# A hybrid decoder layer on one core: TensorE keeps the source's order in the stage of the state-space groups, and the weave of that stage is rewritten

## The chip, the cores and the metric

The kernel runs on 1 core of one Trainium2 chip. The time is device time in microseconds from one launch. The kernel before was timed in three runs, 1043.99, 1045.71 and 1045.89 us, with a median of 1045.71 us. One more execution was taken with the hardware profiler; it took 1044.05 us, of which 1042.2 us lie between its first and its last instruction (the span).

## The reference

One decoder layer on 512 tokens of width 1024, with 16 learned meta tokens ahead of them. All data are fp32.

```python
u = rmsnorm(h, mix_norm_w)
proj = u @ w_in                       # pool | z | xbc | dt | gates
y_pool = pool_mixer(u_pool) @ w_pool_up
y_ssd = mamba2_branch(z, xbc, dt) @ w_ssd_out
h = h + (gate_pool * y_pool + gate_ssd * y_ssd) @ w_o
v = rmsnorm(h, mlp_norm_w)
h = h + (relu(v @ w_ff1) ** 2) @ w_ff2
out = rmsnorm(h, final_norm_w)[16:]
...
# mamba2_branch
xbc = silu(causal_depthwise_conv(xbc))        # x (2048) | B (8x128) | C (8x128)
y = ssd_chunked(x, dt, a, B, C) + x * d_skip  # 4 chunks of 128 tokens, 8 groups
y = y * silu(z)
y = y * rsqrt(mean(y * y over the group's 256 channels) + eps) * norm_w
```

In `ssd_chunked`, for each group of four heads and each chunk, C and B give a masked 128x128 matrix that is weighted by exponentials of summed dt and applied to x (the part inside the chunk), and a running state, built from B and x chunk by chunk, is applied by C (the part from earlier chunks).

## The kernel before

Channels lie on the 128 partitions, tokens along the free dimension. Each fp32 product is made from three products of rounded halves: a weight block of 128x1024 is loaded (`raw`, on SyncE's queue, three buffers), ScalarE copies its rounded upper half (`whi`, L75) and VectorE subtracts to get the lower half (`wlo`, L76), each of the two with four buffers; `proj` (L147 to L153) then issues per 128 rows of the contraction the products whi by upper half (L150), whi by lower half (L151) and wlo by upper half (L153). A projection of 528 tokens takes 48 matmuls into one accumulator of two banks (`px`, L150 to L153), one of 512 tokens 24.

The stage that the change touches is a loop over eight groups g (L577). For each g, `ssd(g)` (L390) is a generator of seven steps, and its steps alternate with those of the projections for the next group, `group_proj(g + 1)` (L359): B (`bt`), C (`ct`) and the two halves of x (`xc`), each a block of 48 matmuls with a convolution of four taps behind it (L340 on ScalarE, L343 three times on VectorE, L345 the Silu on ScalarE), then in some groups a pooling gate (`pgp`, 24 matmuls), then z (`pz`, two blocks, 48 matmuls in all, Silu on ScalarE at L385). In group 4 the first half of the output projection (`pso`, 192 matmuls in eight steps) comes first; in group 7 there is no next group, and the step's partner is the second part of the output projection (`psp`, eight steps of 18 matmuls).

The seven steps of `ssd(g)` are these.

1. TensorE transposes B into `ptb`, the meta tokens of x into `ptm` and x into `ptx` (L407 to L428). ScalarE copies `btok` and the rounded meta tokens `bm` (L409 to L413), VectorE finishes `bm` (L414), and makes `xm`, `xdt` and `xdd` (L418 to L433). The decay factors `eb` and `abc` are exponentials on ScalarE (L439 to L450) with subtractions on both engines.
2. TensorE makes `pcb` from B and C (L455) and the state increments `pst` (L462 for the meta tokens, L464). VectorE masks `pcb` into `cbm` (L457), multiplies it into `abc` (L470, 128x2048) and runs the states: `st` of chunk 1, 2 and 3, each a product (L468) and an addition (L469) on the state before; chunk 0 is a copy on ScalarE (L466).
3. TensorE makes `po`, two halves of four chunks each, from the states (L478), and `py` from `abc` and `xdt` (L484). VectorE combines them into `yt` for the first half (L488 to L492).
4. The same four operations on VectorE for the second half.
5. ScalarE squares `yt` (L496); the square is split into `qh` and `ql`.
6. TensorE sums the squares over the group's channels (`png`, L501 and L502), ScalarE takes the root (L504), VectorE four reciprocals (L506).
7. VectorE scales `yt` (L510), and the result is split into `yh` (L513, ScalarE) and `yl` (L514, VectorE), which the output projections read.

What each engine issues first is not set by this text alone. The layer under the kernel records the operations with their dependencies and gives each engine one fixed sequence, by priorities in the order of the source and by its own estimate of when an operation can start; the tiles' buffers are handed out along with it. Each engine then works through its sequence in order and waits on semaphores. In the kernel before this holds for all engines: TensorE's sequence, too, is the scheduler's, which put matmuls of a following block between the products of `po`, or the whole of z ahead of transposes.

The accumulators of two banks (`psum2`) have two buffers, those of one bank (`psum1`) four.

Of the kernel before, what the change touches and what calls it, by code (L numbers as in the profile page):

```python
# [21 lines left out]
G = 8  # L22
# [19 lines left out]
GATE_AT = {1: 3, 2: 4, 3: 5, 5: 6}  # L42
# [9 lines left out]
def kernel(ctx: ExitStack, tc, xT, x, w, vec, fnw, out):  # L52
# [12 lines left out]
    def block_tiles():  # L65
        b = nblk[0]
        nblk[0] += 1
        return (b, wp.tile([P, 1024], F32, tag="raw", name=f"raw{b}", bufs=3),
                wp.tile([P, 1024], F32R, tag="whi", name=f"whi{b}"),
                wp.tile([P, 1024], F32R, tag="wlo", name=f"wlo{b}"))  # L70

    def block_part(t, c):
        b, raw, hi, lo = t
        nc.sync.dma_start(raw[:, c], w[b, :, c])
        act.copy(hi[:, c], raw[:, c])  # L75
        dve.tensor_tensor(lo[:, c], raw[:, c], hi[:, c].bitcast(F32), op=ALU.subtract)  # L76

    def block():
        t = block_tiles()
        block_part(t, slice(0, 1024))  # L80
        return t[2:]

    def units():

        while True:
            hi, lo = block()
            for j in range(NK):
                yield hi[:, j * P : (j + 1) * P], lo[:, j * P : (j + 1) * P]

    def mm3(ps, a, b, first, last):  # L90
        (ah, al), (bh, bl) = a, b
        pe.matmul(ps, ah, bh, start=first, stop=False)  # L92
        pe.matmul(ps, ah, bl, start=False, stop=False)  # L93
        pe.matmul(ps, al, bh, start=False, stop=last)  # L94
# [45 lines left out]
    def psum2(name):  # L140
        return psa.tile([P, 1024], F32, tag="mm", name=name)
# [4 lines left out]
    def proj_step(outs, k, wblk, rhs):  # L146

        wh, wl = (t[:, k * P : (k + 1) * P] for t in wblk)
        for o, c in outs:
            pe.matmul(o, wh, rhs[0][k][:, c], start=k == 0, stop=False)  # L150
            pe.matmul(o, wh, rhs[1][k][:, c], start=False, stop=False)  # L151
        for o, c in outs:
            pe.matmul(o, wl, rhs[0][k][:, c], start=False, stop=k == NK - 1)  # L153

    def proj(outs, wblk, rhs):
        for k in range(NK):
            proj_step(outs, k, wblk, rhs)

    def wide(ps, skip=0):

        h = (L - skip) // 2
        runs = [(ps[:, 512 - h : 512], slice(skip, skip + h)),
                (ps[:, 512 : 512 + h], slice(skip + h, L))]
        return runs, ps[:, 512 - h : 512 + h]

    def narrow(ps):
        return [(ps, slice(NM, L))]
# [20 lines left out]
    b, raw, hi, lo = wdt  # L188
# [89 lines left out]
    def dtile(name):  # L278
        return dp.tile([P, W], F32, name=name)

    v, e, s, s2, pl, dt, acs = (dtile(n) for n in ("dv", "de", "ds", "ds2", "dpl", "ddt", "dacs"))
# [22 lines left out]
    for c in (slice(0, P), slice(P, W)):  # L304
        n = c.stop - c.start
# [31 lines left out]
    def conv(dst, src, ct):  # L337
        n = dst.shape[-1]
        e = src.shape[-1] - n
        act.activation(dst, src[:, e:], AF.Identity, bias=col(V_CB, ct), scale=col(V_CW, ct * 4 + 3))  # L340
        for j in range(1, 4):
            o = max(0, j - e)
            dve.scalar_tensor_tensor(dst[:, o:], src[:, e + o - j : e + n - j],  # L343
                                     col(V_CW, ct * 4 + 3 - j), dst[:, o:], op0=ALU.mult, op1=ALU.add)
        act.activation(dst, dst, AF.Silu)  # L345

    def group_tiles(g):
        xc = gc.tile([P, 2, L], F32, tag="xc", name=f"xc{g}")
        bt = gc.tile([P, L], F32, tag="bt", name=f"bt{g}")
        ct = gc.tile([P, SEQ], F32, tag="ct", name=f"ct{g}")  # L350
        zt = gc.tile([P, 2, SEQ], F32, tag="zt", name=f"zt{g}", bufs=1)
        return xc, bt, ct, zt

    def first_raw(name, ps, skip):
        r = pre.tile([P, L - skip], F32, tag="raw0", name=f"raw0_{name}", bufs=4)
        act.copy(r, ps)
        dve.tensor_tensor(r, r, rsb[:, skip:], op=ALU.mult)
        return r

    def group_proj(g, cur, gate=None):  # L360

        first = g == 0
        xc, bt, ct, zt = cur
        for dst, t, skip in ((bt, 16 + g, 0), (ct, 24 + g, NM - 4), (xc[:, 0, :], 2 * g, 0),
                             (xc[:, 1, :], 2 * g + 1, 0)):
            if first and dst is bt:
                view = viewB
            else:
                runs, view = wide(psum2(f"px{g}_{t}"), skip)
                proj(runs, block(), X if first else U)  # L370
            conv(dst, first_raw(t, view, skip) if first else view, t)
            yield
        if gate is not None:
            gate_pool(gate)
            yield
        ps = psum2(f"pz{g}")
        for i in range(2):
            proj(narrow(ps[:, i * SEQ : (i + 1) * SEQ]), block(), X if first else U)
        zf = zt.rearrange("p i t -> p (i t)")
        if first:  # L380
            dve.tensor_tensor(zt, ps.rearrange("p (i t) -> p i t", i=2),
                              rsb[:, NM:].unsqueeze(1).to_broadcast([P, 2, SEQ]), op=ALU.mult)
            act.activation(zf, zf, AF.Silu)
        else:
            act.activation(zf, ps, AF.Silu)  # L385
        yield
# [128 lines left out]
            ys.append((yh, yl))  # L515
        yield

    def weave(a, b, n):

        end = object()  # L520
        a = [a]
        while a or b:
            for s in [a] + [b] * n:
                if s and next(s[0], end) is end:
                    s.pop(0)

    def gate_pool(d, first=False):
        ps = psum2(f"pgp{d}")[:, :SEQ]
        proj(narrow(ps), block(), X if first else U)
        if first:  # L530
            dve.tensor_tensor(m1[d], ps, rsb[:, NM:], op=ALU.mult)
        act.activation(m1[d], m1[d] if first else ps, AF.Sigmoid, bias=col(V_BG, d))


    cur = group_tiles(0)
    gp0 = group_proj(0, cur)
    for _ in gp0:
        pass
# [14 lines left out]
    def ssd_out(d, ps, ks):  # L553
        wh, wl = block()
        for n, k in enumerate(ks):
            c = slice(n * P, (n + 1) * P)
            mm3(ps, (wh[:, c], wl[:, c]), ys[k], n == 0, n == len(ks) - 1)

    def out_half():
        for dd in range(4):  # L560
            ps = psum2(f"pso{dd}")
            for i in range(2):
                ssd_out(2 * dd + i, ps[:, i * SEQ : (i + 1) * SEQ], range(8))
                act.copy(acc[2 * dd + i], ps[:, i * SEQ : (i + 1) * SEQ])
                yield

    def out_part():

        un = units()
        for d in range(NK):  # L570
            ps = psum2(f"psp{d}")[:, :SEQ]
            for k in range(8, 14):
                mm3(ps, next(un), ys[k], k == 8, k == 13)
            dve.tensor_tensor(acc[d], acc[d], ps, op=ALU.add)
            yield

    for g in range(G):  # L577
        nxt = group_tiles(g + 1) if g + 1 < G else None
        fill = [group_proj(g + 1, nxt, GATE_AT.get(g))] if nxt else [out_part()]
        if g == 4:  # L580
            fill = [out_half()] + fill
        weave(ssd(g, cur), fill, 2 if g == 4 else 1)
        cur = nxt
    gc_stack.close()


# [63 lines left out]
    for n, gi in enumerate(POOL_ORDER):  # L650
        nxt = []
# [403 lines left out]
    for t in range(4):  # L1055
        T, st = t // 2, slice((t % 2) * P, (t % 2 + 1) * P)
        n = 0
        for half in range(2):
            parts = [(0, 512)] if half == 0 or t < 3 else [(0, 256), (256, 256)]
            for a, m in parts:  # L1060
# [3 lines left out]
                i = 0  # L1064
# [157 lines left out]
```

## Time and profile before

| what | value |
|---|---|
| median of three runs | 1045.71 us |
| the profiled execution | 1044.05 us |
| its span, first to last instruction | 1042.2 us |
| TensorE matmuls busy | 1015.7 us (97%), 5689 |
| VectorE busy | 741.5 us (71%) |
| ScalarE busy | 564.8 us (54%) |
| mean granted TensorE clock | 0.99 |
| DMA | 105.62 MB, 101 GB/s |
| chain that ended last, by engine | PE 84%, DVE 6%, ACT 6%, issue 2% |

PE is TensorE's matmul stream, PEld its weight loads, DVE is VectorE, ACT ScalarE, POOL GpSimd, SP SyncE. In a row of a timeline stand the start in us, the length in us, the engine, the line of the kernel, the operation, the output and inputs by the program's names without buffer numbers, the shapes, the count and, in brackets, the idle time of the engine before it with what ended it. In a row of the waits stand who waited, for what, the total in us, how often, and the longest. In a row of windows stand the stretch, its length, then for PE, PEld, DVE, ACT and POOL the busy time with the number of instructions, the granted clock of TensorE, the share of DMA and GB/s. Matmuls overlap: the rate of a block is read from the distance of starts, not from the length of one.

### The profile page before, as it was taken

What the parts mean: (1) busy time and instruction counts of PE and PEld (TensorE: products, weight loads), DVE (VectorE), ACT (ScalarE), POOL (GpSimd) and SP (SyncE); (2) the same over time, 40 slices, a digit from 0 to 9 for tenths busy, and PEclk for the clock granted to TensorE, in tenths of its full rate; (3) what the DMA queues carried; (4) which work ended last, traced back from release to release, by engine and by line L of the source; (5) the groups of instructions that cost most, each with busy time, mean ns of one, the idle gap of its engine ahead of it and who ended that gap; (6) DMA issues with size and microseconds to landing.
All of it is one profiled execution on the core that took longest, in us unless ns stands there. A gap on an engine that the chain in (4) does not pass through costs nothing.

```text
span 1042.2 us, 14107 instructions
## 1 busy us (share of the span) xinstructions
PE 1015.7 (97%) x5689; PEld 880.9 (85%) x5689; DVE 741.5 (71%) x982; ACT 564.8 (54%) x744; POOL 88.7 (9%) x52
## 2 busy tenths in 40 slices
PE   9999899989899998999999999999999999999997
PEld 8889699879788997978889888888888888888886
DVE  7978777787744686868757456885767666666866
ACT  7776748676725539493234333465455344454444
POOL 0100000000000000000000000001221412404400
PEclk9999999999999999999999999999999999999999
DMA  6242042223133230403533332414323323233112
GB/s 234 81 145 102 6 162 76 102 78 105 66 137 101 82 103 19 163 21 122 203 101 101 101 95 70 160 42 181 102 81 120 98 86 121 85 118 110 47 46 81
DMA packets 29281, 105.62 MB, mean 101 GB/s; under 512 B 3296, under 2 KB 4256, under 8 KB 28192
## 3 DMA queue, kind: packets, MB, share of 16 engines
q1 hardware_dynamic: 26496, 92.75, 27.4%
q0 software_dynamic: 2000, 11.08, 2.8%
q8 instruction: 44, 0.72, 0.3%
q10 hardware_dynamic: 720, 0.91, 0.2%
q14 instruction: 21, 0.17, 0.0%
HBM read 102.55 MB, written 2.16 MB: 100 GB/s over the span
## 4 chain that ended last, share of the span: by engine, by line
PE 84%; DVE 6%; ACT 6%; issue 2%; DMA 0%; SPq 0%; ACTq 0%; DVEq 0%
PE pf L94 6%; PE pf L92 6%; PE pf L93 6%; PE px L150 4%; PE px L151 4%; PE px L153 4%; PE alpha L971 3%; PE alpha L973 3%; PE alpha L972 3%; PE py L484 2%; PE pz L153 2%; PE pz L150 2%; PE pz L151 2%; PE pso L92 2%; PE pp L153 1%
## 5 line engine op out<-in xcount | busy, mean ns | idle before, releaser
L75 ACT CAST whi<-raw 128x1024 fp32r<-128x1024 f32 (+1 forms) x131 | 135.8, 1043 | 235.1 <-PE pf L93 55.8
L76 DVE TENSOR_TENSOR wlo<-raw,whi 128x1024 fp32r<-128x1024 f32 (+1 forms) x131 | 163.3, 1251 | 111.4 <-ACT whi L75 111.4
L150 PE MATMUL px<-uh,whi 128*128 128x264 f32 (+1 forms) x448 | 121.9, 292 | 0.3 <-DVE bt L343 0.3
L151 PE MATMUL px<-ul,whi 128*128 128x264 f32 (+1 forms) x448 | 118.8, 286 | 0.0
L92 PE MATMUL pf<-vh,whi 128*128 128x512 f32 x256 | 99.8, 390 | 0.0
L94 PE MATMUL pf<-vh,wlo 128*128 128x512 f32 x256 | 99.6, 389 | 0.0
L93 PE MATMUL pf<-vl,whi 128*128 128x512 f32 x256 | 99.6, 389 | 0.0
L153 PE MATMUL px<-uh,wlo 128*128 128x264 f32 (+1 forms) x448 | 91.2, 286 | 0.0
L150 PEld LDWEIGHTS px<-uh,whi 128*128 128x128 f32 x448 | 86.0, 192 | 2.0 <-issue 1.5
L151 PEld LDWEIGHTS px<-ul,whi 128*128 128x128 f32 x448 | 85.6, 191 | 0.6 <-issue 0.2
L733 DVE TENSOR_TENSOR slo<-b,shi 128x1024 fp32r<-128x1024 f32 x35 | 49.1, 1404 | 31.6 <-ACT shi L732 27.4
L153 PEld LDWEIGHTS px<-uh,wlo 128*128 128x128 f32 x448 | 69.3, 190 | 0.5 <-DVE wlo L76 0.3
L732 ACT CAST shi<-b 128x1024 fp32r<-128x1024 f32 x35 | 36.7, 1050 | 47.2 <-PE pf L93 36.4
L94 PEld LDWEIGHTS pf<-vh,wlo 128*128 128x128 f32 x256 | 48.1, 188 | 10.0
L93 PEld LDWEIGHTS pf<-vl,whi 128*128 128x128 f32 x256 | 48.1, 188 | 10.0
L92 PEld LDWEIGHTS pf<-vh,whi 128*128 128x128 f32 x256 | 48.1, 188 | 9.8
L982 POOL TENSOR_TENSOR b<-b,b 128x1024 f32<-128x1024 f32 x14 | 35.7, 2547 | 238.3 <-DVE slo L733 210.1
L971 PE MATMUL alpha<-shi,hh 128*128 128x512 f32 x140 | 54.6, 390 | 0.0
L972 PE MATMUL alpha<-slo,hh 128*128 128x512 f32 x140 | 54.5, 389 | 0.0
L973 PE MATMUL alpha<-shi,hl 128*128 128x512 f32 x140 | 54.5, 389 | 0.0
L798 DVE TENSOR_TENSOR ht<-ht,alpha 128x1024 f32<-128x1024 f32 x35 | 42.5, 1215 | 10.9 <-PE alpha L973 10.9
L150 PE MATMUL pz<-uh,whi 128*128 128x512 f32 x112 | 43.9, 392 | 0.0
(419 smaller groups left out, 2539.4 us busy)
## 6 DMA issues: line engine op xcount, KB each, us to landing
raw<-in_w SPq DMA_DIRECT2D x129, 512.0 KB, 3.6
b<-in_w SPq DMA_DIRECT2D x28, 512.0 KB, 3.6
abc<-acs_d POOLq DMA_DIRECT2D x8, 1024.0 KB, 4.9
wob<-in_w SPq DMA_DIRECT2D x8, 512.0 KB, 4.8
xt<-in_xT SPq DMA_DIRECT2D x8, 264.0 KB, 5.4
ht<-in_x POOLq DMA_DIRECT2D x4, 512.0 KB, 6.1
w<-in_w SPq DMA_DIRECT2D x4, 512.0 KB, 3.5
out_dram<-out SPq DMA_DIRECT2D x4, 320.0 KB, 2.4
```

Of the source, the lines that this page charges most:

```text
L75: act.copy(hi[:, c], raw[:, c])
L76: dve.tensor_tensor(lo[:, c], raw[:, c], hi[:, c].bitcast(F32), op=ALU.subtract)
L92: pe.matmul(ps, ah, bh, start=first, stop=False)
L93: pe.matmul(ps, ah, bl, start=False, stop=False)
L94: pe.matmul(ps, al, bh, start=False, stop=last)
L150: pe.matmul(o, wh, rhs[0][k][:, c], start=k == 0, stop=False)
L151: pe.matmul(o, wh, rhs[1][k][:, c], start=False, stop=False)
L153: pe.matmul(o, wl, rhs[0][k][:, c], start=False, stop=k == NK - 1)
L733: dve.tensor_tensor(lo, src, hi.bitcast(F32), op=ALU.subtract)
L971: pe.matmul(ps[t], a[0], wh[:, cs], start=f, stop=False, skip_group_check=True)
L972: pe.matmul(ps[t], a[0], wl[:, cs], start=False, stop=False, skip_group_check=True)
L973: pe.matmul(ps[t], a[1], wh[:, cs], start=False, stop=l, skip_group_check=True)
```

## The change

```diff
@@ group_proj
         ps = psum2(f"pz{g}")
         for i in range(2):
             proj(narrow(ps[:, i * SEQ : (i + 1) * SEQ]), block(), X if first else U)
+            if gate is None and i == 0:
+                yield
@@ weave
-    def weave(a, b, n):
+    def weave(a, b, counts):
 
         end = object()
-        a = [a]
-        while a or b:
-            for s in [a] + [b] * n:
-                if s and next(s[0], end) is end:
-                    s.pop(0)
+        for _, n in zip(a, counts):
+            while n and b:
+                if next(b[0], end) is end:
+                    b.pop(0)
+                else:
+                    n -= 1
+        for rest in [a] + b:
+            for _ in rest:
+                pass
@@ the loop over groups
-    for g in range(G):
-        nxt = group_tiles(g + 1) if g + 1 < G else None
-        fill = [group_proj(g + 1, nxt, GATE_AT.get(g))] if nxt else [out_part()]
-        if g == 4:
-            fill = [out_half()] + fill
-        weave(ssd(g, cur), fill, 2 if g == 4 else 1)
-        cur = nxt
+    STEPS = {4: (2, 2, 2, 2, 1, 2, 3), 7: (2, 2, 1, 1, 1, 1, 0)}
+    with tc.manual_schedule(engines={mybir.EngineType.PE}):
+        for g in range(G):
+            nxt = group_tiles(g + 1) if g + 1 < G else None
+            fill = [group_proj(g + 1, nxt, GATE_AT.get(g))] if nxt else [out_part()]
+            if g == 4:
+                fill = [out_half()] + fill
+            weave(ssd(g, cur), fill, STEPS.get(g, (1, 1, 1, 1, 1, 1, 0)))
+            cur = nxt
```

Within `manual_schedule` TensorE's instructions keep the order of the source; the other engines' sequences are still made by the scheduler, along with it. After step i of `ssd` come `counts[i]` steps of the projections. Where group g has no pooling gate (groups 0, 4 and 6), z is two steps, so that step 6 with `png` falls between the two halves of z. In group 7 two partial projections of the output follow each of the first two steps, and one each of the next four. The operations and their number stay the same; the order of the weight blocks in HBM, too. The lines from 379 on move by 2 to 8.

Three places where the sequences differ follow; names carry their buffer's group (and a running number), so `po0_1` is the second half of group 0's `po`.

TensorE, group 0, the products from the states and the part inside the chunk. Before:

```order
L478 MATMUL po0_0_1026<-ct0_416,st0_0_947 128x128
L478 MATMUL po0_1_1027<-ct0_416,st0_0_947 128x128
L478 MATMUL po0_0_1026<-ct0_416,st1_0_948 128x128
L478 MATMUL po0_1_1027<-ct0_416,st1_0_948 128x128
L484 MATMUL py0_0_1028<-abc0_824,xdt0_826 64x128 x8
```

With the change, at the same place:

```order
L480 MATMUL po0_0_1028<-ct0_416,st0_0_949 128x128
L480 MATMUL po0_0_1028<-ct0_416,st1_0_950 128x128
L480 MATMUL po0_0_1028<-ct0_416,st2_0_951 128x128
L480 MATMUL po0_0_1028<-ct0_416,st3_0_952 128x128
L480 MATMUL po0_1_1029<-ct0_416,st0_0_949 128x128
L480 MATMUL po0_1_1029<-ct0_416,st1_0_950 128x128
L480 MATMUL po0_1_1029<-ct0_416,st2_0_951 128x128
L480 MATMUL po0_1_1029<-ct0_416,st3_0_952 128x128
L486 MATMUL py0_0_1030<-abc0_826,xdt0_828 64x128 x8
L486 MATMUL py0_1_1031<-abc0_826,xdt0_828 64x128 x8
```

The products with the states of chunks 2 and 3 stood behind `py0_0` and 7 and 21 matmuls of the next block; now all eight stand together ahead of `py`. It is so in every group.

ScalarE, group 1 into group 2, around z of group 2 (`whi23` to `whi26` are the blocks of B, C and x for group 3; the block of B is the first one that TensorE needs behind the transposes of group 2). Before:

```order
L450 ACTIVATE abc2_1756<-abc2_1756 128x1024
L513 COPY yh1_0_1743<-yt1_1475 128x512
L513 COPY yh1_1_1748<-yt1_1475 128x512
L449 ACTIVATE abc2_1756<-abc2_1756 128x1024
L385 ACT_TABLE_LOAD
L385 ACTIVATE zt2_1273<-pz2_1680 128x1024
L409 COPY btok2_1760<-ptb2_1761 128x384
L412 COPY bm_114<-ptb2_1761 16x128
L413 COPY bm_114<-ptb2_1761 16x128
L75 COPY whi24_1899<-raw24_1898 128x1024
```

With the change:

```order
L515 COPY yh1_1_1750<-yt1_1477 128x512
L387 ACT_TABLE_LOAD
L387 ACTIVATE zt2_1275<-pz2_1682 128x1024
L411 COPY btok2_1762<-ptb2_1763 128x384
L414 COPY bm_114<-ptb2_1763 16x128
L415 COPY bm_114<-ptb2_1763 16x128
L451 ACT_TABLE_LOAD
L451 ACTIVATE abc2_1758<-abc2_1758 128x1024
L75 COPY whi23_1816<-raw23_1815 128x1024
L75 COPY whi24_1901<-raw24_1900 128x1024
```

`whi23` stood much earlier, right behind the first tap of the last block of x (L340), and now stands behind z, `btok`, `bm` and an exponential. In groups 3, 4 and 6 the first block behind the transposes stands likewise behind z, `btok` and `bm`, with both exponentials ahead of z (there it stood behind them before, too, and TensorE took it up only after `pst`). Two table loads more stand between the split of the square and z in group 1.

VectorE, group 1, from the mask of `pcb` to the third state (`wlo17` is the block of C for group 2, which TensorE takes up right behind `pst`). Before:

```order
L457 TENSOR_TENSOR cbm1_1395<-pcb1_1390,tri_78 128x512
L343 TENSOR_SCALAR bt2_1271<-px2_18_1330,vs_85,bt2_1271 128x525
L468 TENSOR_TENSOR st1_1_1398<-st0_1_1397,cdec_90 128x256
L470 TENSOR_TENSOR abc1_1274<-abc1_1274,cbm1_1395 128x2048
L469 TENSOR_TENSOR st1_1_1398<-st1_1_1398,pst1_0_1401 128x256
L76 TENSOR_TENSOR wlo17_1418<-raw17_1416,whi17_1417 128x1024
L468 TENSOR_TENSOR st2_1_1399<-st1_1_1398,cdec_90 128x256
L76 TENSOR_TENSOR wlo18_1511<-raw18_1509,whi18_1510 128x1024
L469 TENSOR_TENSOR st2_1_1399<-st2_1_1399,pst1_1_1402 128x256
```

With the change:

```order
L459 TENSOR_TENSOR cbm1_1397<-pcb1_1392,tri_78 128x512
L343 TENSOR_SCALAR bt2_1273<-px2_18_1332,vs_85,bt2_1273 128x527
L470 TENSOR_TENSOR st1_1_1400<-st0_1_1399,cdec_90 128x256
L343 TENSOR_SCALAR bt2_1273<-px2_18_1332,vs_85,bt2_1273 128x526
L471 TENSOR_TENSOR st1_1_1400<-st1_1_1400,pst1_0_1403 128x256
L343 TENSOR_SCALAR bt2_1273<-px2_18_1332,vs_85,bt2_1273 128x525
L470 TENSOR_TENSOR st2_1_1401<-st1_1_1400,cdec_90 128x256
L472 TENSOR_TENSOR abc1_1276<-abc1_1276,cbm1_1397 128x2048
L471 TENSOR_TENSOR st2_1_1401<-st2_1_1401,pst1_1_1404 128x256
L76 TENSOR_TENSOR wlo17_1420<-raw17_1418,whi17_1419 128x1024
L470 TENSOR_TENSOR st3_1_1402<-st2_1_1401,cdec_90 128x256
L76 TENSOR_TENSOR wlo18_1513<-raw18_1511,whi18_1512 128x1024
```

The first two taps of the convolution stood ahead of the mask, and the split `wlo17` behind the first state; now the mask comes first, and the split behind the second. The four reciprocals of group 0 (L506), which stood between `xdd` and the last subtraction of `bm` (L414), now stand ahead of the transposes' operations.

In groups 2, 3, 5 and 6 VectorE's sequence has one split of a weight block between L470 and L471 of the third state (L468 and L469 before); before, there was one in groups 2 and 5 there, too. Within the stage SyncE's and GpSimd's queues issue the same transfers in the same order; behind it some loads for w_o stand a few places earlier or later on SyncE's.

## The prediction

> **What bounds the kernel now.** The page shows TensorE (PE) busy for 1015.7 of the 1042.2 us, so I asked first for what PE waits for. The view of waits, for PE alone, gives (who waited, for what: total us, times, longest):
>
> ```profile
> PE pst L464 <- DVE xdd L433: 7.0, 3, 2.3
> PE pst L462 <- DVE xm L422: 3.3, 3, 1.1
> PE pst L462 <- DVE bm L414: 3.2, 2, 2.6
> PE po L478 <- DVE st L469: 2.7, 3, 2.0
> PE po L478 <- DVE cbm L457: 2.2, 1, 2.2
> PE px L150 <- DVE bt L343: 0.3, 1, 0.3
> ```
>
> These sum to 18.7 us and all lie in the groups' stage (66.6 to 503.8 us). By windows they sit in group 1 (5.1), groups 3, 4 and 6 (3.4 each, where pcb and pst follow ptx with nothing between), group 7 (2.6), groups 0 and 2 (0.7 together). Nowhere else does PE wait long, so PE's order is worth these 18.7 us and what they do to the clock:
>
> ```profile
> 100.00:200.00 100.00, 94.63 (x662) 86.74 (x661) 76.89 (x119) 66.97 (x90) 1.05 (x2) 0.97 0.29 95
> 200.00:300.00 100.00, 93.12 (x545) 81.17 (x544) 68.05 (x105) 68.44 (x89) 0.53 (x1) 0.97 0.25 81
> 400.00:500.00 100.00, 93.98 (x568) 81.77 (x567) 76.21 (x113) 63.73 (x84) 0.53 (x1) 0.97 0.26 85
> 119.64:123.05 3.41, 1.85 (x12) 1.53 (x10) 3.41 (x7) 3.41 (x6) 0.00 (x0) 1.00 0.00 0
> 123.05:126.46 3.41, 1.22 (x6) 0.84 (x6) 3.41 (x4) 2.10 (x3) 0.00 (x0) 1.00 0.00 0
> 126.46:133.28 6.82, 6.09 (x30) 5.54 (x31) 5.92 (x10) 1.04 (x1) 0.00 (x0) 0.50 0.51 150
> ```
>
> First number after the stretch: its length; then PE, PEld, DVE, ACT, POOL busy; then the granted clock. Three stretches of 100 us at 0.97 are some 6 to 7 us each at half clock, that is two windows of 3.41 us each, six in all. A window with PE busy for 1.85 us left the next at full clock; one with 1.22 was followed by half clock, which costs half of what PE does there (6.09 / 2 = 3.0 us for the two windows of group 1, at most 3.41 / 2 = 1.7 for each of the other four; I take 8.5 in all). So the stake is at most 18.7 + 8.5 = 27 us. The question is what the new order makes PE wait for.
>
> **What it removes.** In groups 3, 4 and 6 a whole block of 48 matmuls now stands between ptx and pcb, as it does in groups 2 and 5, which waited for 0.3 and nothing: those 10.3 us go. With the norm's sums between the halves of z, the reciprocals come one half earlier, and bm no longer stands behind them in groups 1 and 7 (0.6 and 2.6). I take all 18.7 us away, and add what comes in their place.
>
> **Group 0, the output products.** Before, PE took the chunks of po as their states came, with py and parts of the next block between. Now the four chunks of one half stand together, behind the whole px block. The order of DVE up to there is unchanged, and its states are paced by the convolutions that stand between their steps (the first and the third addition):
>
> ```profile
> 82.53 0.41 DVE L469 TENSOR_TENSOR st<-st,pst 128x256 f32<-128x256 f32 x1
> ...
> 86.51 0.41 DVE L469 TENSOR_TENSOR st<-st,pst 128x256 f32<-128x256 f32 x1
> ```
>
> PE reaches po at 82.0 (before: the same place, the same time). Its fourth chunk waits for 86.92: 4.9 us less three products of 0.28 (six passes in 0.83, below) = 4.1 us. What covered this were py and 21 matmuls of px, which now stand behind.
>
> **Groups 2, 3, 5 and 6, the same place.** DVE's order has a weight split between the last two state steps. Its slot comes free only when the px block on PE ends:
>
> ```profile
> 182.60 1.05 ACT L75 CAST whi<-raw 128x1024 fp32r<-128x1024 f32 x1 [2.51 <-PE px L151]
> ```
> ```profile
> 185.19 0.41 DVE L469 TENSOR_TENSOR st<-st,pst 128x256 f32<-128x256 f32 x1
> ```
> ```profile
> 174.62 1.05 PE L455 MATMUL pcb<-ct,bt 128*128 128x128 f32 x8
> ...
> 176.74 0.47 PE L150 MATMUL px<-uh,whi 128*128 128x258 f32 x1
> ...
> 182.64 0.83 PE L478 MATMUL po<-ct,st 128*128 128x128 f32 x6
> ```
>
> PE's fourth chunk is due at 182.64 + 0.8 = 183.4; the state can be there at 182.60 + 1.05 + 1.21 (the split, below) + 0.41 less 0.1 of overlap = 185.2 (before: 185.6). That is 1.8 us, four times: 7.2. (In group 4 a block of 11 us and in group 7 two of 4.2 stand before po: nothing.)
>
> **Group 1, the split of the ct block.** Before, DVE stood so:
>
> ```profile
> 122.92 0.68 DVE L457 TENSOR_TENSOR cbm<-pcb,tri 128x512 f32<-128x512 f32 x1
> 123.52 0.75 DVE L343 SCALAR_TENSOR_TENSOR bt<-px,vs,bt 128x525 f32<-128x525 f32 x1
> 124.19 0.41 DVE L468 TENSOR_TENSOR st<-st,cdec 128x256 f32<-128x256 f32 x1
> 124.52 2.28 DVE L470 TENSOR_TENSOR abc<-abc,cbm 128x2048 f32<-128x2048 f32 x1
> 126.72 0.41 DVE L469 TENSOR_TENSOR st<-st,pst 128x256 f32<-128x256 f32 x1
> 127.06 1.21 DVE L76 TENSOR_TENSOR wlo<-raw,whi 128x1024 fp32r<-128x1024 f32 x1
> ```
>
> Now cbm comes first, then three bt, four st and abc, then this split: by the steps from start to start 0.60 + 3 x 0.67 + 4 x 0.33 + 2.20 + 1.21 = 7.3 us from the end of pcb. PE has pst to do (176.74 - 175.67 = 1.1) and four matmuls of the block (5.9 / 48 = 0.12 each), so it stands for 7.3 - 1.6 = 5.7 us at the first L153. It was no better before (5.1 in this group); the wait only changes its name.
>
> **Groups 2, 3, 4 and 6, the first block behind ptx.** This is the largest term. ScalarE (ACT) now copies that block's upper half (whi) after everything that hangs on z and ptb. In group 2 before:
>
> ```profile
> 151.52 1.04 ACT L75 CAST whi<-raw 128x1024 fp32r<-128x1024 f32 x1
> 152.58 1.28 ACT L439 ACT_TABLE_LOAD   x1
> ...
> 167.63 1.06 ACT L449 ACTIVATE abc<-abc 128x1024 f32<-128x1024 f32 x1
> 168.70 1.28 ACT L385 ACT_TABLE_LOAD   x1
> 170.00 1.02 ACT L385 ACTIVATE zt<-pz 128x1024 f32<-128x1024 f32 x1
> 170.92 0.47 ACT L409 COPY btok<-ptb 128x384 f32<-128x384 f32 x1
> ```
>
> No row from 150.3 to 172.9 has an idle time before it: ACT is full. The new order takes whi (1.06) and the second exponential (1.07) out ahead of zt and puts two table loads in (2 x 1.29): zt at 170.45. Behind it come btok (0.92 later), the two bm (0.9 together), a table load (1.3), the exponential (1.0) and then whi (1.04): 175.6. I take 1.2 off, since one split of 1.2 no longer stands between the yt rows on DVE that ACT's queue starts from: 174.4. PE wants it here:
>
> ```profile
> 167.27 0.49 PE L407 MATMUL ptb<-ident,bt 128*128 128x128 f32 x3
> ...
> 168.72 0.37 PE L150 MATMUL px<-uh,whi 128*128 128x264 f32 x1
> ```
>
> 5.7 us, and the lower half (wlo, 1.2 us on DVE after whi) comes 0.7 after the four matmuls that do without it: 6.4. In groups 3, 4 and 6 the exponential stands ahead of zt without a load of its own. From group 3's rows:
>
> ```profile
> 218.19 1.02 ACT L385 ACTIVATE zt<-pz 128x1024 f32<-128x1024 f32 x1
> 219.11 0.61 ACT L513 CAST yh<-yt 128x512 fp32r<-128x512 f32 x1
> ```
>
> zt at 218.19 - 0.89 (btok and bm go behind) + 0.97 = 218.27, whi ready 3.5 later (0.92 + 0.63 + 0.9 + 1.03) at 221.7, less the same 1.2 = 220.5. z ends at 216.56 and PE wants the block 1.45 later, at 218.0: 2.5 + 0.8 = 3.3 us, three times 9.9. What hid this until now was the wait for pst itself: px stood behind it. In group 7 the second block of weights stands there instead, 24 matmuls later: 1.8 us, an estimate by the same steps.
>
> By the Trainium skill (ScalarE: Activation LUTs, What ACT_TABLE_LOAD costs) a switch is the 1283 ns load plus a drain of 1380 ns. The trace agrees with the load (1.28) and shows no drain: the next instruction starts 0.02 us after it. By the page the two further loads and the one behind bm would make group 2's term 4 us longer.
>
> **The sum.** 4.1 + 7.2 + 5.7 + 6.4 + 9.9 + 1.8 = 35.1 us come, 18.7 go: +16.4. Half-clock windows: the waits of groups 0, 1 and 2 exceed 2.2 us in a window for certain (one or two each), the three of 2.5 + 0.8 about every second time, those of 1.8 hardly: some six, as now, so nothing. The profiled execution took 1044.05 us: 1044.05 + 16.4 = **1060.5 us**. It lies 1.7 below the median of the runs shown (1045.71), and I leave it there.
>
> The DMAs cost nothing: in the stage SP's queue issues the same blocks in the same order, and raw copies of the late blocks were asked for long before; abc on POOL's queue goes out when py has read the one before, and two px blocks of 5.9 us begin between that and the first exponential on it; if that cover were gone, ACT would start later by the rest.
>
> Bounds: group 0 by one convolution step of 0.75 (3.3 to 4.3); group 1 by one split of 1.2 (4.5 to 6.9); the first blocks from zt at the very end of z (4.4, and 2.8 three times) to no 1.2 taken off (7.6, and 4.5 three times); po 1.4 to 2.2, four times; group 7 nothing to 3.3. Together 26.2 to 44.3, that is +7.5 to +25.6. Two clock windows more or fewer are 3 us either way: 1048.5 to 1072.7.
>
> **Rivals.**
> (a) *The splits are early enough* (faster). If DVE and ACT, which also get PE's idle time, run ahead of z in every group, only the po waits of groups 0, 2, 3, 5 and 6 stay, 11.3 us, too short for the clock: 1044.05 - 18.7 - 8.5 + 11.3 = 1028. For it: ACT is busy for only 64 to 68 of 100 us. Against: it is full in just the stretch before whi. It decides if whi stands less than 1.5 us behind the end of z, where the order gives 5 and more. 6%.
> (b) *The clock falls with each wait.* If also the 1.8 us waits and all of 3.3 bring a half-clock window, there are some 13 instead of 6: 7 x 1.5 = 10 us more, 1071. For it: nobody knows where between 1.56 and 2.19 us of idle time the limit lies. 15%.
> (c) *The clock needs a whole idle window.* Then only the waits near 6 us count, one window each: two in place of six, 4 x 1.5 less, 1054.5. Against: 1.22 us of work in the window before did not keep the clock. The Trainium skill has this rule (TensorE: Matmul & The Clock Gate, Part 1: The HAM clock gate): cold after an idle window of about 3.4 us; the trace agrees with the length of the window, not with a wholly idle one. 6%.
> (d) *Even*: half of the waits for first blocks are hidden and the clock is better by three windows: 1060.5 - 8 - 5 = 1047.5, and with the lowest values about 1044. 6%.
>
> **How the numbers follow.** My case has 67%. Range 1048 to 1073 holds it, (b), (c) and part of (d). About 0.2%, 2 us, is what a measurement of this kernel can tell from no change: faster 0.07 (a, and a little of d), same 0.04, slower 0.89.
>
> **What would show it.** Right: PE waits at px L150 for ACT whi and at L153 for DVE wlo in groups 1, 2, 3, 4 and 6, the longest in groups 1 and 2 (5 to 6 us each); po waits for st in groups 0, 2, 3, 5 and 6; no wait of pst for xdd. PE's idle time in the stage near 35 us. Wrong: whi of group 2's first block copied within 1.5 us of the end of z, or po without waits.

## The result, and the profile after

| | time, us (median) | profiled execution, us | span, us | TensorE idle, 66 to 520 us | windows at half clock there |
|---|---|---|---|---|---|
| before | 1045.80 | 1044.05 | 1042.2 | 18.7 | 6 |
| with the change | 1074.03 (1073.43 to 1076.6, 4 runs) | 1073.43 | 1071.7 | 40.0 | 13 |

The ratio to the kernel before is 1.0278 (95% interval 1.0257 to 1.0298): slower, as forecast, but by 28 us where 16 were forecast, and 1 us above the upper end of the range. TensorE's busy time on the page:

```profile
PE 1023.4 (95%) x5689; PEld 887.6 (83%) x5689; DVE 742.6 (69%) x982; ACT 564.8 (53%) x744; POOL 88.6 (8%) x52
```

The work is the same (5689 matmuls), yet PE is busy for 7.7 us more than before (1023.4 against 1015.7). Matmuls that run at half clock are longer, so the clock already shows here. The waits of PE after the change:

```profile
PE px L150 <- ACT whi L75: 10.5, 4, 5.3
PE po L480 <- DVE st L471: 9.8, 7, 1.5
PE px L153 <- DVE wlo L76: 8.7, 3, 4.8
PE pso L92 <- ACT acc L570: 4.9, 4, 1.4
PE pso L92 <- ACT whi L75: 2.3, 1, 2.3
PE pso L94 <- DVE wlo L76: 2.0, 1, 2.0
...
PE psp L93 <- DVE yl L516: 0.8, 1, 0.8
PE psp L94 <- DVE wlo L76: 0.5, 1, 0.5
PE psp L92 <- ACT whi L75: 0.4, 1, 0.4
```

Of the names of before only one is left, po for st, with 9.8 us in seven waits where it had 2.7 in three: no pst for xdd, xm or bm, no po for cbm, no px for bt. In their place stand the splits of the weights (whi, wlo), these states in front of po, and one name that the prediction did not have, acc. Group 2 shows the longest wait; ACT stands without a pause behind zt until it comes to the block's upper half:

```profile
172.58 1.02 ACT L387 ACTIVATE zt<-pz 128x1024 f32<-128x1024 f32 x1
...
175.69 1.06 ACT L451 ACTIVATE abc<-abc 128x1024 f32<-128x1024 f32 x1
176.65 2.92 ACT L75 CAST whi<-raw 128x1024 fp32r<-128x1024 f32 x3
...
177.73 0.59 PE L150 MATMUL px<-uh,whi 128*128 128x264 f32 x1 [5.33 <-ACT whi L75]
```

The idle time of PE comes from one row of the view of windows per kernel, of before and of the change (454.00 less the PE column):

```profile
66.00:520.00 454.00, 435.32 (x2865) 391.04 (x2864) 328.11 (x502) 278.11 (x367) 3.70 (x7) 0.98 0.29 98
```
```profile
66.00:520.00 454.00, 414.00 (x2693) 372.08 (x2692) 306.99 (x473) 267.21 (x354) 3.70 (x7) 0.95 0.25 86
172.88:176.29 3.41, 0.00 (x0) 0.00 (x0) 2.95 (x7) 3.37 (x6) 0.00 (x0) 1.00 0.00 0
176.29:179.71 3.42, 1.97 (x7) 1.66 (x8) 2.00 (x2) 3.29 (x4) 0.00 (x0) 0.50 0.00 0
179.71:183.12 3.41, 3.41 (x17) 3.41 (x17) 1.50 (x2) 0.56 (x1) 0.00 (x0) 0.50 0.79 286
230.91:234.32 3.41, 0.75 (x4) 0.54 (x4) 3.28 (x7) 3.37 (x6) 0.00 (x0) 1.00 0.00 0
234.32:237.73 3.41, 2.27 (x10) 2.27 (x11) 3.36 (x3) 0.24 (x1) 0.00 (x0) 0.50 0.37 73
251.39:254.80 3.41, 1.86 (x15) 1.48 (x14) 3.27 (x7) 1.72 (x2) 0.00 (x0) 1.00 0.06 7
254.80:258.21 3.41, 3.41 (x29) 3.18 (x29) 2.77 (x5) 0.63 (x1) 0.00 (x0) 0.50 0.48 147
459.60:463.01 3.41, 1.86 (x15) 1.48 (x13) 3.27 (x7) 1.72 (x2) 0.00 (x0) 1.00 0.00 0
463.01:466.42 3.41, 3.41 (x44) 3.12 (x45) 3.41 (x6) 0.31 (x1) 0.00 (x0) 1.00 0.41 159
```

The last three columns are clock, DMA share and GB/s; the clock of a row is what the row before earned. Group 2's stall leaves a window without any work: the next is at 0.50. In that next window the stall is not over (1.97 us busy), so the one after it is at 0.50, too: two windows for one stall. Group 3 shows the same with 0.75 and 2.27. The 1.55 us of idle time for po from 251 us on leave 1.86 us of work and still cost one window; the same 1.86 at 459.6 us cost none.

**One sum for the whole time.** If a half-clock window costs half of PE's busy time in it, the span less idle time less that cost must be the same in every kernel with this work. It is 1013.8 before and 1013.9 with the change, and stays within 1009.3 to 1013.9 in all kernels below (some 16 us of spare matmuls taken off where there are any). Columns 3 and 4 are taken over the trace between 66 and 520 us, the last column from unrounded figures:

| kernel | span | PE idle | half-clock windows, PE busy in them | span - idle - half of that |
|---|---|---|---|---|
| before | 1042.2 | 18.7 | 6, 19.5 | 1013.8 |
| the change | 1071.7 | 40.0 | 13, 35.5 | 1013.9 |
| order_alone | 1084.4 | 47.3 | 17, 47.9 | 1013.1 |
| steps_alone | 1030.4 | 13.9 | 2, 6.6 | 1013.2 |
| keep_busy | 1063.7 | 28.1 | 4, 12.0 | 1029.7 (1013.7 without the spare matmuls) |
| look1 | 1034.0 | 18.1 | 3, 9.0 | 1011.4 |
| low_late | 1058.7 | 31.3 | 10, 29.7 | 1012.5 |
| acc_late | 1066.4 | 34.9 | 14, 39.1 | 1011.9 |
| py_first | 1058.9 | 34.5 | 10, 27.4 | 1010.7 |
| comb4 | 1022.8 | 10.5 | 1, 3.4 | 1010.7 |
| comb5 | 1017.0 | 6.1 | 1, 3.1 | 1009.3 |
| look1_free | 1015.6 | 2.2 | 0 | 1013.4 |
| comb6 | 1010.2 | 0.8 | 0 | 1009.5 |

So the 29.5 us of span are 21.3 of idle time and 8.0 of clock, with 0.2 left over. Counted without the clock, span less idle time would run from 1009.5 (comb6) to 1037.1 (order_alone). The four kernels with py ahead of po (py_first, comb4, comb5, comb6) have the four lowest remainders, 1009.3 to 1010.7; the other nine lie between 1011.4 and 1013.9.

### The profile page after: what moved, and what is told of

The parts are those of the page before. It is cut to its first block, busy times and chain, and to the rows that moved or that the text cites. A ratio compares the mean times of both kernels' runs of the same rounds, so it can differ in the third digit from the quotient of the medians.

```text
span 1071.7 us, 14100 instructions
## 1 busy us (share of the span) xinstructions
PE 1023.4 (95%) x5689; PEld 887.6 (83%) x5689; DVE 742.6 (69%) x982; ACT 564.8 (53%) x744; POOL 88.6 (8%) x52
## 4 chain that ended last, share of the span: by engine, by line
PE 85%; DVE 6%; ACT 6%; issue 2%; DMA 1%; SPq 0%; DVEq 0%; ACTq 0%
PE pf L92 5%; PE pf L93 5%; PE pf L94 5%; PE px L150 5%; PE px L153 5%; PE px L151 5%; PE alpha L979 3%; PE alpha L980 3%; PE alpha L981 3%; PE pz L153 2%; PE pz L150 2%; PE pz L151 2%; DVE wlo L76 2%; PE py L486 1%; PE pp L151 1%
## 5 line engine op out<-in xcount | busy, mean ns | idle before, releaser
L150 PE MATMUL px<-uh,whi 128*128 128x264 f32 (+1 forms) x448 | 124.5, 298 | 10.5 <-ACT whi L75 10.5
L151 PE MATMUL px<-ul,whi 128*128 128x264 f32 (+1 forms) x448 | 121.9, 292 | 0.0
L153 PE MATMUL px<-uh,wlo 128*128 128x264 f32 (+1 forms) x448 | 94.8, 294 | 8.7 <-DVE wlo L76 8.7
L150 PEld LDWEIGHTS px<-uh,whi 128*128 128x128 f32 x448 | 89.0, 199 | 12.9 <-ACT whi L75 11.6
L151 PEld LDWEIGHTS px<-ul,whi 128*128 128x128 f32 x448 | 88.5, 198 | 0.2
L153 PEld LDWEIGHTS px<-uh,wlo 128*128 128x128 f32 x448 | 72.6, 198 | 9.7 <-DVE wlo L76 9.7
L740 ACT CAST shi<-b 128x1024 fp32r<-128x1024 f32 x35 | 36.7, 1049 | 47.3 <-PE pf L93 36.4
L508 DVE RECIPROCAL rs<-rs 128x128 f32<-128x128 f32 x32 | 27.2, 911 | 28.8 <-ACT rs L506 28.8
```

## The experiments

Times are medians of 4 runs, ratios are to the kernel before on the same chip.

**Which half of the change costs?** order_alone has the fixed order with the old steps, steps_alone the new steps with the order left to the scheduler (both against the change; order_alone also has the old `weave` back, and in steps_alone the loop moves out one level):

```diff
 order_alone
-    STEPS = {4: (2, 2, 2, 2, 1, 2, 3), 7: (2, 2, 1, 1, 1, 1, 0)}
...
-            if gate is None and i == 0:
-                yield
...
-            weave(ssd(g, cur), fill, STEPS.get(g, (1, 1, 1, 1, 1, 1, 0)))
+            weave(ssd(g, cur), fill, 2 if g == 4 else 1)
 steps_alone
-    with tc.manual_schedule(engines={mybir.EngineType.PE}):
```

> Half of the change: TensorE keeps the source's order, but the source has the old order of steps (z in one piece, one step of the projections after each step of a group, so png stands behind the whole of z). Theory (TensorE's fixed order is the cause, since the weight splits stay late on ACT and DVE): the waits of px for whi and wlo and of po for st are there as with the whole change, together 25 to 30 us, and the wait for bm behind the reciprocals stays in groups 1 and 7 (about 3 us): 1071 to 1079 us. Rival (the new places of png and of the partial projections are what costs): at most 1050 us, and no wait of px for whi over 1 us.

> The other half: the new order of steps (z in two pieces, png between them, two partial projections a step at the end), but TensorE's sequence is left to the scheduler as before. Theory: no wait of px for whi over 1 us, groups 3, 4 and 6 keep their waits of pst for xdd (about 2 us each), the wait for bm is shorter: 1041 to 1049 us, five to seven windows of half clock. Rival (the steps are the cause): 1060 us or more.

order_alone: 1082.9 us, 1.0364 (1.0338 to 1.0391). steps_alone: 1034.6 us, 0.9907 (0.9882 to 0.9932). Both lie outside the ranges that were expected, each on the side of the theory. The waits of order_alone, then of steps_alone:

```profile
PE px L153 <- DVE wlo L76: 10.9, 3, 7.0
PE po L478 <- DVE st L469: 10.8, 9, 1.5
PE px L150 <- ACT whi L75: 10.0, 3, 5.3
PE psp L92 <- ACT yh L513: 5.0, 1, 5.0
```
```profile
PE pst L466 <- DVE xdd L435: 7.0, 3, 2.3
PE pst L464 <- DVE xm L424: 3.3, 3, 1.1
PE pst L464 <- DVE bm L416: 2.7, 1, 2.7
...
PE po L480 <- DVE st L471: 0.4, 1, 0.4
```

The fixed order alone brings whi, wlo and po. With the old steps it is dearer still: in group 1 PE waits 7.0 us for the split, because cbm, which stands ahead of it on DVE, starts 3.9 us after the last products of pcb (126.70 against 122.83 us in the timeline), behind the norm's products with yt, two taps of bt and both yl, and in group 7 psp waits for yh behind the late norm (5.0). The steps alone are a gain of 11 us: 4.8 us less idle time and four half-clock windows less (half of 19.5 less 6.6, 6.5). The change thus joins a part that gains 11 us with one that costs 39 on top of it (1074.0 against 1034.6).

**Does the clock cost what the sum says?** Spare matmuls stand where PE waits, so that it waits busily:

```diff
+    KEEP = {17: 32, 23: 32, 30: 24, 37: 24, 58: 24}
+    def keep(ps):
+        for _ in range(KEEP.get(nblk[0] - 1, 0)):
+            pe.matmul(ps[:, :256], ones_r, uh[0][:, NM : NM + 256], start=True, stop=True)
     def proj(outs, wblk, rhs):
+        keep(outs[0][0])
...
     def ssd_out(d, ps, ks):
         wh, wl = block()
+        keep(ps)
```

> The changed kernel with spare matmuls (128x256, result overwritten) at the places where TensorE waits for weights: 32 ahead of the blocks of B for group 3 (in group 2) and of C for group 2 (in group 1), 24 ahead of the first blocks in groups 3, 4 and 6; by 0.12 us each 3.9 and 2.9 us, less than the wait that they stand in. What is waited for comes no sooner. Theory (each wait of 4 to 6 us also costs two windows at half clock, 1.0 to 1.5 us each): eight to ten of the 13 windows go, 1060 to 1066 us although TensorE has 136 matmuls more to do. Rival (the waits cost only their own length): 1072 us or more, by as much as the spare matmuls exceed the waits.

1066.1 us, 1.0205 (1.0185 to 1.0224): 8 us less than the change, though PE does 136 matmuls more; that is at the edge of the expected range. Nine half-clock windows went. Its row of the view of windows:

```profile
66.00:520.00 454.00, 425.94 (x2861) 384.36 (x2860) 309.87 (x478) 269.96 (x357) 3.71 (x7) 0.98 0.26 87
```

Idle time fell by 11.9 and the clock's cost by 11.8 (17.8 to 6.0), while the spare matmuls took some 16 (136, one start every 0.12 us): -8 by the sum, -8.0 of span measured. Had waits cost only their length, the time would have grown by 16 - 11.9 = 4 us. This shows the clock's price apart from the waits'.

**Are late splits the cause of the waits for whi and wlo?** `look[0]` is 1 within the stage and 0 elsewhere, so that each block is asked for one ahead.

```diff
+    ahead, look = [], [0]
+
     def block():
-        t = block_tiles()
-        block_part(t, slice(0, 1024))
-        return t[2:]
+        while len(ahead) < 1 + look[0]:
+            t = block_tiles()
+            block_part(t, slice(0, 1024))
+            ahead.append(t[2:])
+        return ahead.pop(0)
...
+    look[0] = 1
     STEPS = {4: (2, 2, 2, 2, 1, 2, 3), 7: (2, 2, 1, 1, 1, 1, 0)}
...
+    look[0] = 0
     gc_stack.close()
```

> The changed kernel, but in the groups' stage each weight block is asked for and split one block ahead in the source, so that whi of the first block behind ptx stands on ACT ahead of z, and wlo17 on DVE ahead of the taps of bt. TensorE's order stays. Theory: the waits for whi and wlo (10.5 + 8.7 + some 4.8 in group 4) go, with eight to ten windows of half clock: 1073.4 - 22 - 10 = 1041, 1037 to 1048 us; the waits of po for st (9.8) and of pso for acc (4.9) stay. Rival (ACT and DVE are simply full there, and what is moved ahead pushes z, bm and xdd late by as much): 1060 us or more, with waits of pst or px for those in their place.

1035.5 us, 0.9911 (0.9892 to 0.993): better than expected, and better than before.

```profile
PE po L484 <- DVE st L475: 9.7, 7, 1.6
PE pso L96 <- ACT acc L574: 4.1, 4, 1.4
PE px L157 <- DVE wlo L76: 2.4, 1, 2.4
```

The waits of px and pso for whi are gone, px waits for wlo only in group 1 (2.4), and po and acc stay nearly as they were. Idle time falls by 21.9 us and ten of 13 windows go. So there was room on ACT and DVE; what was wrong was the place in their queues. The loads of the raw blocks are issued a block earlier, too, but in the change PE's long wait in group 2 was not for a load: ACT has no pause ahead of that whi (rows above). Nothing else came late in exchange: pst and px have no new waits.

**The second wait of a stall.** Within the stage all products of a projection (`proj`; pso and psp stay as they were) with the upper half come first:

```diff
+    late = [0]
+
     def proj(outs, wblk, rhs):
+        if not late[0]:
+            for k in range(NK):
+                proj_step(outs, k, wblk, rhs)
+            return
+        wh, wl = wblk
         for k in range(NK):
-            proj_step(outs, k, wblk, rhs)
+            for o, c in outs:
+                pe.matmul(o, wh[:, k * P : (k + 1) * P], rhs[0][k][:, c], start=k == 0, stop=False)
+                pe.matmul(o, wh[:, k * P : (k + 1) * P], rhs[1][k][:, c], start=False, stop=False)
+        for k in range(NK):
+            for o, c in outs:
+                pe.matmul(o, wl[:, k * P : (k + 1) * P], rhs[0][k][:, c], start=False, stop=k == NK - 1)
...
+    late[0] = 1
...
+    late[0] = 0
```

> The changed kernel, but in the groups' stage each projection does its 32 matmuls with the upper half of the block first and the 16 with the lower half behind them, so that wlo is wanted 3.9 us after whi and not 0.5. The number of matmuls stays. Theory (after the wait for whi comes a second one for wlo, which falls into a half-clock window and keeps the clock down for a second window): the waits of px for wlo (8.7) go, those for whi (10.5) stay, and the second windows of the pairs in groups 1, 2, 3 and 6 go: 1073.4 - 8.7 - 4 x 1.0 = 1061, 1057 to 1065 us. Rival (DVE has no room there, so wlo comes later by as much and the wait stands in the middle of the block): 1069 us or more.

1055.9 us, 1.0107 (1.0074 to 1.014), below the expected range, and for other reasons than expected:

```profile
PE po L492 <- DVE st L483: 18.2, 11, 2.9
PE px L165 <- ACT whi L75: 5.4, 2, 3.6
```

px no longer waits for wlo, and with DVE and ACT in another order even the waits for whi are halved; but po waits for st nearly twice as long. In DVE's order two splits and a tap of ct now stand between the state steps of groups 1 to 3 (in the change, in group 2, one split). About second windows it decides nothing, since several waits changed at once (ten windows are left where nine were expected). Its runs also differ more than the others' (1053.5 to 1060.6 us), and the profiled one is the longest of them.

**The wait that was not foreseen.**

```diff
                 ssd_out(2 * dd + i, ps[:, i * SEQ : (i + 1) * SEQ], range(8))
-                act.copy(acc[2 * dd + i], ps[:, i * SEQ : (i + 1) * SEQ])
+                if i == 1:
+                    for j in range(2):
+                        act.copy(acc[2 * dd + j], ps[:, j * SEQ : (j + 1) * SEQ])
                 yield
```

> The changed kernel, but the two halves of each pso are copied to acc together, after the second half, so that the second half's matmuls no longer stand behind the copy of the first on ACT. Theory (the wait that the prediction did not see): pso's waits for acc, 4.9 us, go or fall under 1.5: 1067 to 1070 us. Rival (the wait is for the buffer and only moves to pso2 and pso3 or to px5, which then wait for two copies): 1072 us or more.

1068.7 us, 1.0224 (1.0207 to 1.0242), as expected. The row "pso <- ACT acc" is gone from the waits, the others stand nearly as they were; idle time fell by 5.1 to 34.9, while one half-clock window more came (14). The wait was that of the second half of a pso for the copy of the first, which stands behind a split on ACT. In the changed kernel's timeline:

```profile
301.64 1.04 ACT L75 CAST whi<-raw 128x1024 fp32r<-128x1024 f32 x1 [2.88 <-PE pso L93]
302.59 0.58 ACT L570 COPY acc<-pso 128x512 f32<-128x512 f32 x1
...
303.22 0.50 PE L92 MATMUL pso<-yh,whi 128*128 128x512 f32 x1 [1.39 <-ACT acc L570]
```

**The waits of po.** The loop over py is put ahead of the one over po:

```diff
         for i in range(2):
             for c in range(4):
-                pe.matmul(po[i][:, c * P : (c + 1) * P],
-                          flat(st[c])[:, i * P : (i + 1) * P], ct[:, ctok(c)], start=True, stop=True)
-        for i in range(2):
-            for c in range(4):
                 for j in range(2):
...
                               xdt[:, c, r, :], dm[:, r, c, :], start=True, stop=True)
+        for i in range(2):
+            for c in range(4):
+                pe.matmul(po[i][:, c * P : (c + 1) * P],
+                          flat(st[c])[:, i * P : (i + 1) * P], ct[:, ctok(c)], start=True, stop=True)
```

> The changed kernel with the 16 products of py ahead of the eight of po in every group. py needs abc times cbm, which DVE does ahead of the last state step, and takes 2.5 us. Theory: the 1.5 us waits of po for st in groups 2, 3, 5 and 6 go and that of group 0 falls from 3.7 to about 1.2: 8.6 us, and the three half-clock windows behind them (87, 255 and 405 us) with 1.0 each: 1062, 1059 to 1065 us. Rival (py then waits for abc as long as po did for st): 1070 us or more.

1060.1 us, 1.0142 (1.0127 to 1.0157), in the range. po's row falls from 9.8 to 1.8:

```profile
PE px L150 <- ACT whi L75: 15.9, 3, 5.3
PE pso L92 <- ACT whi L75: 5.3, 1, 5.3
...
PE px L153 <- DVE wlo L76: 4.8, 1, 4.8
PE po L486 <- DVE st L471: 1.8, 2, 1.5
```

Idle time fell by 5.5, not by 8.6, because whi came later in groups 3, 4 and 6 (now up to 5.3 us in one piece instead of 2.3 and 2.0); what that took was made up by three half-clock windows fewer and some 3 us that the sum leaves open. The windows that went are not the three that were expected: those at 255 and 405 us did, that at 87 us stayed, and one in group 1 went instead. Most of the 3 us lie in the two products themselves: from start to start, weighted with the granted clock and without idle time, po and py take 33.0 us of PE in the change and 30.2 here. Why is not shown.

This run also has stalls in one piece, with no wait for wlo behind them. Group 3's is one wait of 5.30 us, and two windows are at half clock:

```profile
229.99 0.59 PE L150 MATMUL px<-uh,whi 128*128 128x264 f32 x1 [5.30 <-ACT whi L75]
```
```profile
223.68:227.09 3.41, 1.01 (x10) 0.77 (x8) 3.29 (x9) 3.37 (x6) 0.00 (x0) 1.00 0.00 0
227.09:230.50 3.41, 0.51 (x2) 0.51 (x3) 1.65 (x3) 3.40 (x4) 0.00 (x0) 0.50 0.00 0
230.50:233.92 3.42, 3.41 (x16) 3.10 (x15) 2.97 (x3) 1.33 (x2) 0.00 (x0) 0.50 0.46 145
```

It is so in groups 2, 3, 4 and 6 of this run, while the 4.84 us of group 1 fell into one window for the most part (0.43 us of work left in it, all of the next one full) and cost one.

**Together, and without the fixed order.** comb4 is look1, acc_late and py_first in one; comb5 adds low_late; comb6 is comb4 without `manual_schedule`, look1_free is look1 without it.

> The three cures together on the changed kernel: weight blocks one ahead, both halves of pso copied together, py ahead of po. Theory (what is left are the three waits by name): look1's 1035.5 less 8.5 for po, 4.1 for acc and two to three windows: 1021, 1018 to 1026 us. Rival (the waits hide one another; with one gone the next stands in its place): 1029 us or more.

> The three cures together and the lower halves of each block last, all on the changed kernel. What is left of waits in the run with the three cures is 10.5 us, 2.4 of it for wlo in group 1 with the one half-clock window near it. Theory (by the sum that holds for all runs so far: 1013 us and some 2 around the span, plus TensorE's idle time in the stage, plus half of its busy time in half-clock windows): the 2.4 go and the waits of po stay covered by py: 1018 to 1024 us. Rival (the lower halves come out of DVE later still and po waits longer behind them, as po did with the lower halves last alone, 18.2 us): 1027 us or more.

> The three cures and the new order of steps, but TensorE's sequence left to the scheduler. Theory (the fixed order costs nothing once what it waits for is made ahead, and gains nothing either: a block of px or psp stands between ptx and pcb in both): within 5 us of the same kernel with the fixed order, 1019 to 1029 us. Rival 1 (the scheduler's order still hides more, po and parts of blocks interleaved): 1018 us or less. Rival 2 (the fixed order is what removed pst's wait for xdd in groups 3, 4 and 6): that wait is back with 7 us and three windows, 1030 us or more.

> The weight blocks one ahead and the new order of steps, without the other two cures, TensorE's sequence left to the scheduler. Theory (the two other cures only mend what the fixed order brings: po's waits and pso's): no wait of po for st over 1 us and none of pso for acc, 1019 to 1028 us, against 1035.5 for the same kernel in the fixed order. Rival (po and pso wait in the free order, too): 1032 us or more.

| | us | ratio (95%) |
|---|---|---|
| comb4 | 1024.3 | 0.9798 (0.9783 to 0.9813) |
| comb5 | 1018.9 | 0.9750 (0.9733 to 0.9766) |
| look1_free | 1017.3 | 0.9741 (0.9726 to 0.9755) |
| comb6 | 1012.3 | 0.9692 (0.9677 to 0.9706) |

comb4 and comb5 fall in their ranges. comb6 is rival 1: 11 to 12 us better than the same kernel in the fixed order (by the ratios and by the medians), so the order costs even when what it waits for is made ahead. look1_free lies just below its theory's range, 18 us under look1: po waits for 0.6 us, pso not at all. In both free orders the waits of pst for xdd, xm and bm, 13 us in steps_alone, are gone as well, so rival 2 of comb6 fails, too. The windows of look1_free and of comb6:

```profile
66.00:520.00 454.00, 451.83 (x3027) 407.28 (x3026) 341.55 (x523) 278.63 (x373) 3.70 (x7) 1.00 0.32 103
```
```profile
66.00:520.00 454.00, 453.23 (x3071) 410.98 (x3070) 344.87 (x528) 287.75 (x381) 3.70 (x7) 1.00 0.31 105
```

In comb6 PE is idle for 0.8 us of the stage and never at half clock. Of the kernels tried it is the fastest, 3.1% under the kernel before.

## Why the prediction was too low

The sign and the mechanism held, and so did the sum of the waits that were foreseen; the count of half-clock windows failed, and one wait was missing.

| term | predicted, us | measured idle, us |
|---|---|---|
| waits removed | 18.7 | 18.7 (po for st, 2.7 of them, is counted anew below) |
| group 0, po | 4.1 | 3.7 |
| groups 2, 3, 5, 6, po | 4 x 1.8 | 4 x 1.55 |
| group 1, split of the ct block | 5.7 | 5.3 |
| group 2, first block behind ptx | 6.4 | 5.3 |
| groups 3, 4, 6, first block | 3 x 3.3 | 4.3, 4.3, 4.2 |
| group 7 | 1.8 | 1.8 |
| sum of what comes | 35.1 | 35.1 |
| pso for acc, group 4 | not foreseen | 4.9 |
| clock | 0 | 8.0 |

That the sum came out at 35.1 is luck in part: the first blocks of groups 3, 4 and 6 were 1 us each too short in the forecast, nearly all others too long. The 1.8 of group 7 agree by chance: only 0.9 of them are waits for the second block's whi and wlo, and 0.8 are a wait for yl, which the forecast did not have. In group 3:

```profile
231.62 2.94 ACT L75 CAST whi<-raw 128x1024 fp32r<-128x1024 f32 x3
232.72 0.39 PE L150 MATMUL px<-uh,whi 128*128 128x264 f32 x1 [2.31 <-ACT whi L75]
...
234.19 3.49 DVE L76 TENSOR_TENSOR wlo<-raw,whi 128x1024 fp32r<-128x1024 f32 x3
235.46 0.81 PE L153 MATMUL px<-uh,wlo 128*128 128x264 f32 x2 [1.99 <-DVE wlo L76]
```

The wait for whi is 2.3 (2.5 was said), but DVE takes up wlo 1.5 us after whi is there, so the second wait is 2.0 and not 0.8.

**The step that failed** is "some six, as now, so nothing", the count of half-clock windows. It was 13, and cost 8.0 us more than before. Groups 0, 1 and 2 had five, within the one or two each that were said. The first blocks of groups 3, 4 and 6 had six, where every second one was to have one, and the waits of po in groups 2, 3, 5 and 6 had two, where there were to be none. The rows above show how: a stall of 4 to 5 us goes on into the next window, which is at half clock already and does not get full either, so that the five stalls of groups 1, 2, 3, 4 and 6 bring two windows each. keep_busy shows that the price of the windows is real. A second wait is not needed for the second window: in py_first stalls in one piece of 5.3 us have two as well, and one of 4.8 that lay mostly in one window has one. Where a stall falls among the windows is not in the forecast, and it is chance in part: in acc_late, which differs in group 4 alone, nearly the same waits of group 0 cost two windows and not one, since the windows' edges lay elsewhere (84.88 us there, 87.55 in the change).

Rival (b), which had 13 windows for the price of 10 us and said 1071, had the right number at 15%, but not for its reason: it let each of the four 1.8 us waits bring a window, and only two did; the pairs make up for the rest. That is luck, too.

**The second miss** is the absent term of 4.9 us, pso for acc. In the forecast group 4 had only its first block. The source's order runs the second half of a pso straight behind its first, and the first half's copy stands in ACT's queue behind a split; before, the scheduler put other products of pso in between (29 of them had ended when the first copy started, where 24 make a half). acc_late shows the term alone. 16.4 + 4.9 + 8.0 = 29.3, against 29.5 of span. Neither miss alone would have left the range: 1060.5 + 8.0 = 1068.5, 1060.5 + 4.9 = 1065.4, both together 1073.4. The bounds allowed the clock two windows either way, not seven, and had no room for a wait that was not named. (Their upper terms add up to 44.4, not 44.3; it changes nothing.)

**The rest.** Rival (a), that the splits are early enough, is refuted by the rows of L150 and L153; rival (c), that only a wholly idle window lowers the clock, by the windows with 0.75 and 1.86 us of work. By the Trainium skill (TensorE: Matmul & The Clock Gate, Part 1: The HAM clock gate) the clock falls after at least one idle window of about 3.4 us and is back after a busy one; the traces agree with the length and with the return, and not with the word idle. That the two table loads cost their 1.28 us and no drain held: in group 2 zt starts 0.01 us after the load. That the DMAs cost nothing held, too; no wait of PE in the stage ends on one.

Left open is why two windows with 1.86 us of work were followed by half clock and one by full, why po and py cost less PE time with py first, and the 2.5 us by which the remainders of the nine other kernels differ.

## What to carry to other kernels

A fixed order on one engine must be read together with the queues that the scheduler then builds for the others: each place where it wants something is checked against where that stands in its producer's queue, for both halves of what it wants and for the buffer it writes into. For a wait, price its length and, window by window, what it does to the clock of the work behind it; here that was 8.0 of 29.5 us. Where a queue holds its work in the wrong place, asking for it one step earlier in the source was worth 17 us in the free order (1034.6 to 1017.3) and 39 in the fixed one (1074.0 to 1035.5), as much as the fixed order had cost, with the same work on the engines.

## What the hardware showed that was not expected

- In all thirteen traces, from 10 to 520 us, each of the 40 full-clock windows with at most 1.47 us of PE work was followed by half clock, and none with 1.90 or more was; of 25 in between, 12 were. PE's busy time as the trace has it is thus not quite what decides.
- A window at half clock gives the full clock back only if PE is busy for nearly all of it: of those windows with less than 3 us of work none did (28, the fullest with 2.95), with 3.11 and more all but one (3.15 in py_first). A short wait that falls into a half-clock window can thus cost one window more.
- Matmuls of 264 columns start every 0.12 us at full clock and every 0.22 at half, so the sum above takes the loss in proportion to the work that stands in the window; that an empty one costs nothing by itself was not tried alone.
